# Splitting float32 weights into two float32r parts: by the vector and scalar engines, or by a casting and an adding DMA

## The chip, the cores and the metric

The kernel runs on one core of one Trainium2 chip. The metric is device time in microseconds (us) of one execution, as the median of several runs. A profile of one execution stands beside it. PE is the engine that multiplies matrices, DVE the vector engine, ACT the scalar engine, POOL the GpSimd engine; SP only issues DMAs here. Every engine runs its own instructions strictly in order.

## The reference, cut to what matters

Two layers of a decoder block over 272 tokens (16 learned ones ahead of 256) of 1024 channels. All weights and activations are float32.

```python
for l in range(2):
    h = rms_norm(x, norm1_g[l])
    u = h @ w_in[l]                       # 1024 x 6560, split among the mixers and their gates
    y_a = conv_module(u_conv, ...)        # gated depthwise convolution, layer norm, projection
    y_b = mla(c_q, c_kv, k_rope, ...)     # latent attention, 8 heads
    y_c = hgrn2(hq, hf, hi, hg, ...)      # gated linear recurrence, 4 heads
    mix = gates[0] * y_a + gates[1] * y_b + gates[2] * y_c
    x = x + mix @ w_out[l]                # 1024 x 1024
    h2 = rms_norm(x, norm2_g[l])
    x = x + square(relu(h2 @ w_ff1[l])) @ w_ff2[l]    # 1024 x 4096 and back
return x[:, 16:]
```

## The kernel before

Tokens lie along the free dimension, channels on the 128 partitions. Weights are packed on the host into blocks of 128 partitions by 1024 float32 columns (512 KB), here called *pieces*; all products with weights go piece by piece. There are 276 of them: per layer 51 of `w_in`, 2 of `w_uq`, 1 of `w_ukv`, 12 of the three branch projections, 8 of `w_out`, 32 of `w_ff1` and 32 of `w_ff2`.

To multiply in float32r and keep the accuracy, each weight and each activation is held as a high part (rounded to float32r) and a low part (the rest), and `mm3` (lines 207 to 210) adds three products into one PSUM bank: high weight by high activation (line 208), low weight by high activation (209), high weight by low activation (210). A piece has eight blocks of 128 columns, so it takes 24 matmuls of 272 columns each (256 in nearly all of layer 1, where the first 16 tokens are dropped).

`piece` (line 193) makes the parts. `fetch` (line 104) loads the raw piece by a DMA from SP into `wraw`, of which there are three buffers. ACT copies it, rounding, into `whi` (line 198). DVE subtracts, `wraw - whi`, into `wlo` (line 200). `whi` and `wlo` have four buffers each. The raw buffer comes free when DVE has subtracted; `whi` and `wlo` when the last matmul of the piece has read them. These steps run at a higher priority than their place in the program (`AHEAD`), and a scheduler sets the order in which each engine's instructions stand; the semaphores follow from that order.

In each layer a mixer stage comes first: pieces of `w_in` and of the branch projections, with the attention, recurrence and convolution steps woven in. Then comes a dense stage: `w_out`, `w_ff1`, `w_ff2`, 72 pieces in which PE does nearly nothing else. POOL does small work only: constants at the start, powers of -1/2 for the norms (`rsqrt`, line 213, and line 806), and memsets and copies in the recurrence (lines 660, 703, 754).

At the start SP loads `xT` in four parts and, in between, the first two blocks of `w_in` (lines 113 to 116), the second of which is handed to `piece` as `raw`.

Of the kernel before, what the change touches and what calls it, by code (L numbers as in the profile page):

```python
# [45 lines left out]
# Column tiles of w_in, in the order in which they are computed.  # L46
# [19 lines left out]
# Columns of the block of per-partition parameters (per layer).  # L66
# [9 lines left out]
# Columns of the block of constants.  # L76
# [10 lines left out]
def block_kernel(ctx, tc, xT_d, pp_d, cc_d, win_d, wuq_d, wukv_d, wbr_d, wout_d, wff1_d, wff2_d, out_d):  # L87
# [15 lines left out]
    # ---------------------------------------------------------------- inputs and constants  # L103
    def fetch(src, n=1024):
        raw = wsp.tile([P, 1024], F32, name="wraw", tag="wraw")
        nc.sync.dma_start(out=raw[:, :n], in_=src[:, :n])
        return raw
# [3 lines left out]
    with tc.high_priority(offset=2 * AHEAD):  # L111
        nc.scalar.dma_start(out=pp, in_=pp_d)
        for j in range(4):
            nc.sync.dma_start(out=xT[:, 2 * j:2 * j + 2, :], in_=xT_d[:, 2 * j:2 * j + 2, :])
            if j == 0:
                first = {"kr": fetch(win_d[0, 0], KD * ROPE), "kv": fetch(win_d[0, 1])}
# [60 lines left out]
    # ---------------------------------------------------------------- helpers  # L177
# [15 lines left out]
    def piece(src, raw=None):  # L193
        """1024 columns of weights, as their high and low parts in float32r."""
        with tc.high_priority(offset=AHEAD):
            raw = raw or fetch(src)
            hi = wsp.tile([P, 1024], F32R, name="whi", tag="whi", bufs=4)
            act.copy(out=hi, in_=raw)  # L198
            lo = wsp.tile([P, 1024], F32R, name="wlo", tag="wlo", bufs=4)
            dve.tensor_tensor(out=lo, in0=raw, in1=hi.bitcast(F32), op=SUB)  # L200
        return hi, lo
# [13 lines left out]
    def spread_rows(r, dst, wins, t0):  # L215
        """dst[:, t - t0] = r of token t on every partition; r holds a column for each window of tokens."""
# [10 lines left out]
    def rms_spread(sq, wcol, wins, t0, rtile=None):  # L227
        """1 / sqrt(eps + the sum over the partitions of sq * wcol) for each token, on every partition."""
# [15 lines left out]
    def add_square(dst, x, k):  # L244
        """dst becomes, or gains, x * x."""
# [11 lines left out]
    def scale_input(xg, l, k):  # L257
        """x * g, before the first norm's division."""
# [5 lines left out]
    # ---------------------------------------------------------------- lower bounds of the second layer  # L264
# [14 lines left out]
    # ---------------------------------------------------------------- layers  # L279
    for l in range(DEPTH):  # L280
# [5 lines left out]
        # h = RMSNorm(x) * g  # L286
# [51 lines left out]
        # ------------------------------------------------------------ u = h @ w_in  # L338
        tiles = win_tiles()
        def win_acc(j, n0):  # L340
            hi, lo = piece(win_d[l, j], first["kv"] if l == 0 and j == 1 else None)
# [17 lines left out]
        def rope_keys(j):  # L359
            """The shared rotary keys: 32 columns, as four sums of two of the eight terms, on 32 partitions each."""  # L360
# [58 lines left out]
        # ------------------------------------------------------------ latent projections  # L419
# [110 lines left out]
        # ------------------------------------------------------------ attention  # L530
        def attention_steps():
# [7 lines left out]
            def finish(w, po):  # L539
                """The heads' outputs for the queries of a tile, with the channels on the partitions."""  # L540
# [37 lines left out]
            def scores(w, c):  # L578
                """Of a pair of heads: exp(q k - max) / its sum."""
# [28 lines left out]
            def turned(w, pr):  # L608
                """The weights of a head, with the keys on the partitions."""
# [29 lines left out]
        # ------------------------------------------------------------ HGRN2  # L639
        def hgrn_steps():  # L640
# [16 lines left out]
            # weights of the keys s in a tile for the queries t of the same tile  # L657
# [11 lines left out]
            for hp in range(2):  # L669
# [4 lines left out]
                # blocks of 8 tokens  # L674
# [22 lines left out]
                # the later half of a block of 16, 32 or 64 tokens against its earlier half  # L697
# [32 lines left out]
                # chunks of 64 tokens against earlier chunks  # L730
# [367 lines left out]
```

## Time and profile before

| | us |
|---|---|
| time, median of 3 runs (lowest to highest) | 965.31 (964.18 to 965.49) |
| span of the profiled execution | 965.4 |
| PE busy | 954.1 |
| DVE busy | 709.2 |
| ACT busy | 521.3 |
| POOL busy | 47.0 |

The span runs from the first to the last instruction of the profiled execution; it is also all that the profile gives of that execution's own time. It stands 0.1 us above the median, within the runs' own spread, so nothing that lies around the span needs to be added. An engine's busy time is the time its instructions took; a DMA issue and a wait are not counted. The profile's windows show, for a stretch of the span, how often a line ran, TensorE's granted clock (1.00 is 2.4 GHz, 0.50 is 1.2 GHz), the mean busy share of the core's 16 DMA engines and the rate at which they moved bytes.

### The profile page before, as it was taken

How to read it: one execution, taken by the hardware profiler on the slowest of the kernel's cores; microseconds unless marked ns; L12 is line 12 of the kernel's file. 1: busy time of each engine (PE TensorE's matmuls, PEld its weight loads, DVE VectorE, ACT ScalarE, POOL GpSimd, SP SyncE). 2: the span in 40 equal slices, each digit the busy share in tenths (PEclk: the TensorE clock that was granted, in tenths of full speed). 3: DMA queues.
4: the chain of work that ended last, by engine and by line, in shares of the span. 5: the costliest groups of instructions: out<-in, count | busy, mean ns of one | idle time of the engine just before them, and what ended most of it. 6: DMA issues, size and time to landing. Idle time of an engine off the chain costs nothing.

```text
span 965.4 us, 18801 instructions
## 1 busy us (share of the span) xinstructions
PE 954.1 (99%) x7578; PEld 906.3 (94%) x7578; DVE 709.2 (73%) x1315; ACT 521.3 (54%) x941; POOL 47.0 (5%) x73
## 2 busy tenths in 40 slices
PE   7999999999999999999999999999999999999998
PEld 6989988888999999999999899888899999999998
DVE  6888998874887866655557899989759887765552
ACT  6575765543536655544436576665445566563331
POOL 2103100000000000000000021000000000000000
PEclk9999999998999999999999999999999999999999
DMA  8444333332455555555554444333334565556561
GB/s 276 149 141 153 110 111 109 110 114 84 154 173 176 175 174 176 175 175 174 175 180 153 131 154 152 107 114 111 131 122 164 161 202 192 188 184 194 192 202 60
DMA packets 42423, 149.18 MB, mean 155 GB/s; under 512 B 4704, under 2 KB 6368, under 8 KB 42336
## 3 DMA queue, kind: packets, MB, share of 16 engines
q1 hardware_dynamic: 40608, 146.10, 46.8%
q10 hardware_dynamic: 1728, 1.88, 0.6%
q8 instruction: 59, 0.97, 0.4%
q14 instruction: 28, 0.23, 0.1%
HBM read 146.91 MB, written 1.05 MB: 153 GB/s over the span
## 4 chain that ended last, share of the span: by engine, by line
PE 96%; DVE 2%; DMA 2%; ACT 1%; issue 0%; ACTq 0%
PE acc L208 18%; PE acc L210 18%; PE acc L209 18%; PE hx L208 9%; PE hx L210 9%; PE hx L209 9%; PE sm L633 2%; PE mx L588 1%; PE pt L612 1%; PE hx L714 1%; DVE wlo L200 1%; PE sm L473 1%; PE hx L797 1%; DMA wraw<-in_win_dram 1%; PE mx L836 1%; PE hx L796 1%
## 5 line engine op out<-in xcount | busy, mean ns | idle before, releaser
L200 DVE TENSOR_TENSOR wlo<-wraw,whi 128x1024 fp32r<-128x1024 f32 x276 | 337.6, 1224 | 183.8 <-ACT whi L198 183.0
L198 ACT CAST whi<-wraw 128x1024 fp32r<-128x1024 f32 x276 | 289.2, 1049 | 338.6 <-PE acc L210 187.6
L208 PE MATMUL acc<-hhi,whi 128*128 128x272 f32 (+1 forms) x704 | 208.0, 296 | 0.0
L209 PE MATMUL acc<-hhi,wlo 128*128 128x272 f32 (+1 forms) x704 | 204.3, 290 | 0.0
L210 PE MATMUL acc<-hlo,whi 128*128 128x272 f32 (+1 forms) x704 | 203.7, 290 | 0.0
L208 PEld LDWEIGHTS acc<-hhi,whi 128*128 128x128 f32 x704 | 133.7, 190 | 7.9 <-issue 4.8
L210 PEld LDWEIGHTS acc<-hlo,whi 128*128 128x128 f32 x704 | 133.5, 190 | 3.1 <-issue 1.7
L209 PEld LDWEIGHTS acc<-hhi,wlo 128*128 128x128 f32 x704 | 133.9, 190 | 1.6 <-issue 0.6
L829 DVE SCALAR_TENSOR_TENSOR cacc<-hpad,pph,cacc 128x272 f32<-128x272 f32 (+1 forms) x240 | 110.3, 486 | 0.3
L210 PE MATMUL acc<-xlo,whi 128*128 128x272 f32 (+1 forms) x256 | 73.1, 286 | 0.0
L208 PE MATMUL acc<-xhi,whi 128*128 128x272 f32 (+1 forms) x256 | 73.1, 286 | 0.0
L210 PE MATMUL hx<-xlo,whi 128*128 128x272 f32 (+1 forms) x256 | 73.0, 285 | 0.0
L209 PE MATMUL hx<-fhi,wlo 128*128 128x272 f32 (+1 forms) x256 | 72.9, 285 | 0.0
L208 PE MATMUL hx<-xhi,whi 128*128 128x272 f32 (+1 forms) x256 | 72.9, 285 | 0.0
L209 PE MATMUL acc<-xhi,wlo 128*128 128x272 f32 (+1 forms) x256 | 72.9, 285 | 0.0
L209 PE MATMUL hx<-xhi,wlo 128*128 128x272 f32 (+1 forms) x256 | 72.9, 285 | 0.0
L209 PE MATMUL acc<-fhi,wlo 128*128 128x272 f32 (+1 forms) x256 | 72.9, 285 | 0.0
L208 PE MATMUL acc<-fhi,whi 128*128 128x272 f32 (+1 forms) x256 | 72.8, 284 | 0.0
L208 PE MATMUL hx<-fhi,whi 128*128 128x272 f32 (+1 forms) x256 | 72.8, 284 | 0.0
L210 PE MATMUL hx<-flo,whi 128*128 128x272 f32 (+1 forms) x256 | 72.7, 284 | 0.0
L210 PE MATMUL acc<-flo,whi 128*128 128x272 f32 (+1 forms) x256 | 72.7, 284 | 0.0
L208 PEld LDWEIGHTS acc<-xhi,whi 128*128 128x128 f32 x256 | 48.3, 189 | 0.1
(344 smaller groups left out, 2115.6 us busy)
## 6 DMA issues: line engine op xcount, KB each, us to landing
wraw<-in_wff_dram SPq DMA_DIRECT2D x128, 512.0 KB, 4.2
wraw<-in_win_dram SPq DMA_DIRECT2D x102, 512.0 KB, 3.4
wraw<-in_wbr_dram SPq DMA_DIRECT2D x24, 512.0 KB, 3.3
wraw<-in_wout_dram SPq DMA_DIRECT2D x16, 512.0 KB, 3.4
wraw<-in_wuq_dram SPq DMA_DIRECT2D x4, 512.0 KB, 3.8
xT<-in_xT_dram SPq DMA_DIRECT2D x4, 272.0 KB, 5.1
wraw<-in_wukv_dram SPq DMA_DIRECT2D x2, 512.0 KB, 3.8
out_dram<-xT ACTq DMA_DIRECT2D x8, 128.0 KB, 3.6
```

The source lines that it names most:

```text
L198: act.copy(out=hi, in_=raw)
L200: dve.tensor_tensor(out=lo, in0=raw, in1=hi.bitcast(F32), op=SUB)
L208: pe.matmul(out, whi, xhi, start=start, stop=False)
L209: pe.matmul(out, wlo, xhi, start=False, stop=False)
L210: pe.matmul(out, whi, xlo, start=False, stop=stop)
L473: pe.matmul(sums[32 * h:32 * h + 32, :L], sel96[:QK, g, :], msq_[:QK, h, :], start=(g == 0), stop=(g == 1))
L588: pe.matmul(sh, qT[h // 4][:, h % 4, WIN[w]:WIN[w] + P], kT[h // 4][:, h % 4, :nk], start=True, stop=False)
L612: pe.transpose(pt[:WROWS[kw], 2 - kw, :], pr[:, WIN[kw]:WIN[kw] + WROWS[kw]], ident)
L633: pe.matmul(place(po, h, P), vv[kw][:WROWS[kw], h * VD:(h + 1) * VD], pts[h % 2][:WROWS[kw], 2 - kw, :], start=(kw == 0), stop=(kw == w))
L714: pe.matmul(ps[:, w - 1, h, :], kl[:, h, WIN[w]:WIN[w] + P], ql[:, h, q0:q0 + 64], start=True, stop=True)
L796: pe.matmul(o, at[w][:, h, :], vtok[w][:, hc], start=True, stop=False)
L829: dve.scalar_tensor_tensor(out=a, in0=hpad[:, c, T0 + k:T0 + k + N], scalar=hpar(l, "cw", c * CK + k), in1=a, op0=MUL, op1=ADD)
```

## The change

The raw pieces are no longer brought on chip. POOL issues a DMA from HBM straight into `whi`; since source and destination differ in type (float32, float32r), this DMA casts on the way. ACT then writes `-whi` into `wlo`, and POOL issues a second DMA from the same place in HBM that adds onto `wlo`, which leaves weight minus high part there. `whi` and `wlo` have five buffers each instead of four. DVE's subtraction is gone. `wraw` is left with one small buffer, for the 256 columns of the rotary keys that SP still loads. The first piece is no longer fetched ahead by SP. Comments and docstrings are gone too, with the line numbers kept.

```diff
     def fetch(src, n=1024):
-        raw = wsp.tile([P, 1024], F32, name="wraw", tag="wraw")
+        raw = wsp.tile([P, KD * ROPE], F32, name="wraw", tag="wraw", bufs=1)
         nc.sync.dma_start(out=raw[:, :n], in_=src[:, :n])
         return raw
...
             if j == 0:
-                first = {"kr": fetch(win_d[0, 0], KD * ROPE), "kv": fetch(win_d[0, 1])}
+                first = {"kr": fetch(win_d[0, 0], KD * ROPE)}
...
-    def piece(src, raw=None):
-        """1024 columns of weights, as their high and low parts in float32r."""
+    def piece(src):
+
         with tc.high_priority(offset=AHEAD):
-            raw = raw or fetch(src)
-            hi = wsp.tile([P, 1024], F32R, name="whi", tag="whi", bufs=4)
-            act.copy(out=hi, in_=raw)
-            lo = wsp.tile([P, 1024], F32R, name="wlo", tag="wlo", bufs=4)
-            dve.tensor_tensor(out=lo, in0=raw, in1=hi.bitcast(F32), op=SUB)
+            hi = wsp.tile([P, 1024], F32R, name="whi", tag="whi", bufs=5)
+            nc.gpsimd.dma_start(out=hi, in_=src)
+            lo = wsp.tile([P, 1024], F32R, name="wlo", tag="wlo", bufs=5)
+            act.activation(out=lo, in_=hi.bitcast(F32), func=AF.Copy, scale=-1.0)
+            nc.gpsimd.dma_start(out=lo, in_=src, accum_op=ADD)
         return hi, lo
...
-            hi, lo = piece(win_d[l, j], first["kv"] if l == 0 and j == 1 else None)
+            hi, lo = piece(win_d[l, j])
```

On POOL, near the start of the program, the constants end and the first norm's power (`r`, line 213) follows. Before (names are tiles; "waits" names whose semaphore is waited for):

```order
L663 MEMSET at_1130 16x64
L146 MEMSET d_126 128x1 [waits Pool_49]
L146 MEMSET d_126 128x1 x4
L162 CAST causal<-stage 128x128 [waits DMAHW4_49]
L163 CAST masks<-stage 128x640
L213 TENSOR_TENSOR r_195<-me,mhalf 128x3 [waits DVE_49]
L213 TENSOR_TENSOR ra<-ra,mhalf 128x6 [waits DVE_49]
```

And with the change, on the same engine at the same place (five issues of `whi` and two of `wlo` stand further up):

```order
L124 COPY ident_101<-ident 32x32 x2
L164 CAST identb<-ident 128x128 [waits Pool_49]
L200 DMA wlo<-in_win_dram 128x1024 [waits Activation_49]
L200 DMA wlo<-in_win_dram 128x1024 [waits DMASW0_49,Activation_49]
L200 DMA wlo<-in_win_dram 128x1024 [waits DMASW1_49,Activation_49]
L162 CAST causal<-stage 128x128 [waits DMAHW1_49]
L163 CAST masks<-stage 128x640
L213 TENSOR_TENSOR r_193<-me,mhalf 128x3 [waits DVE_49]
L197 DMA whi<-in_win_dram 128x1024 [waits DMASW2_49,PE_49]
L200 DMA wlo<-in_win_dram 128x1024 [waits DMASW5_49,DMASW3_49,Activation_49]
L197 DMA whi<-in_win_dram 128x1024 [waits DMASW4_49,PE_49]
```

The first norm's power now stands behind five issues of low parts, each of which waits for ACT, and each later issue of a high part waits for PE to free its buffer.

On POOL, around the dense stage of layer 0, there was nothing to do: between the second norm's inputs (line 806, then `r`) and the first memset of layer 1 (`qq`, line 352) no row stands:

```order
L806 TENSOR_TENSOR ss<-ss,mhalf 16x4 [waits DVE_49]
L806 TENSOR_TENSOR ss<-ss,mhalf 128x4 [waits DVE_49] x2
L213 TENSOR_TENSOR r<-me,mhalf 128x3 [waits DVE_49]
L352 MEMSET qq 128x4x16 [waits DVE_49,PE_49,Activation_49]
L660 MEMSET at_6969 128x512
```

Now the issues for 72 pieces stand there, two for each. In these rows of `w_ff1`, a piece's low part has its high part's number plus two (`whi_3927` and `wlo_3929` are one piece), and the pieces follow each other in steps of 35:

```order
L197 DMA whi_3822<-in_wff1_dram 128x1024 [waits DMASW7_49,PE_49]
L200 DMA wlo_3789<-in_wff1_dram 128x1024 [waits DMASW0_49,Activation_49]
L197 DMA whi_3857<-in_wff1_dram 128x1024 [waits DMASW1_49,PE_49]
L197 DMA whi_3892<-in_wff1_dram 128x1024 [waits DMASW2_49,PE_49]
L200 DMA wlo_3824<-in_wff1_dram 128x1024 [waits DMASW3_49,Activation_49]
L200 DMA wlo_3859<-in_wff1_dram 128x1024 [waits DMASW4_49,Activation_49]
L197 DMA whi_3927<-in_wff1_dram 128x1024 [waits DMASW5_49,PE_49]
L200 DMA wlo_3894<-in_wff1_dram 128x1024 [waits DMASW6_49,Activation_49]
L197 DMA whi_3962<-in_wff1_dram 128x1024 [waits DMASW7_49,PE_49]
L197 DMA whi_3997<-in_wff1_dram 128x1024 [waits DMASW0_49,PE_49]
L200 DMA wlo_3929<-in_wff1_dram 128x1024 [waits DMASW1_49,Activation_49]
```

The high part of a piece is issued one or two pieces ahead of its neighbour's low part: `wlo_3929` stands behind `whi_3997`, which belongs to the piece after the next.

On ACT in the same stage, a piece's rounding copy stood between the two activations of one tile of `w_ff1` (`rl`, line 966, and its square `fhi`, line 967) and those of the next. Before:

```order
L198 CAST whi_4620<-wraw_4618 128x1024 [waits DMAHW1_49,PE_49]
L966 ACTIVATE rl_4505<-acc_4480 128x272 [waits DVE_49]
L967 ACTIVATE fhi_3824<-rl_4505 128x272 [waits Activation_49]
L198 CAST whi_4656<-wraw_4654 128x1024 [waits DMAHW2_49,PE_49]
L966 ACTIVATE rl_4541<-hx_4516 128x272 [waits DVE_49]
```

With the change:

```order
L199 ACTIVATE wlo_4664<-whi_4662 128x1024 [waits DMASW6_49,DMASW1_49]
L966 ACTIVATE rl_4587<-hx_4562 128x272 [waits DVE_49,PE_49]
L967 ACTIVATE fhi_3750<-rl_4587 128x272 [waits Activation_49]
L199 ACTIVATE wlo_4699<-whi_4697 128x1024 [waits DMASW2_49,DMASW0_49]
L966 ACTIVATE rl_4622<-acc_4597 128x272 [waits DVE_49,PE_49]
```

The negating copy takes the place of the rounding one; it waits for two DMAs (the high part's landing, and that of the low part that had the buffer before) where the rounding one waited for a DMA and PE.

## Rows read from the trace of the kernel before

**Rows 1.** The page, busy time of each engine, share of the span, instructions.

```profile
PE 954.1 (99%) x7578; PEld 906.3 (94%) x7578; DVE 709.2 (73%) x1315; ACT 521.3 (54%) x941; POOL 47.0 (5%) x73
```

**Rows 2.** The page, the chain that ended last, share by engine.

```profile
PE 96%; DVE 2%; DMA 2%; ACT 1%; issue 0%; ACTq 0%
```

**Rows 3.** PE's waits: line waited for, us in total, times, longest.

```profile
PE hx L368 <- DVE wkr L364: 6.1, 1, 6.1
PE hx L208 <- DVE gate L889: 0.9, 1, 0.9
```

**Rows 4.** Windows for line 198: length, ACT busy (times), clock, DMA share, GB/s.

```profile
0.00:20.00 20.00, 6.26 (x6) 1.00 0.85 286
20.00:100.00 80.00, 22.21 (x22) 1.00 0.47 147
100.00:230.00 130.00, 28.05 (x27) 0.97 0.33 108
230.00:270.00 40.00, 11.56 (x11) 1.00 0.46 149
270.00:485.00 215.00, 74.36 (x71) 1.00 0.54 174
485.00:545.00 60.00, 18.87 (x18) 1.00 0.48 161
545.00:665.00 120.00, 30.30 (x29) 1.00 0.39 127
665.00:745.00 80.00, 21.20 (x22) 1.00 0.42 134
745.00:950.00 205.00, 75.36 (x72) 1.00 0.59 186
```

**Rows 5.** The page, costliest groups: busy us, mean ns, idle before.

```profile
L200 DVE TENSOR_TENSOR wlo<-wraw,whi 128x1024 fp32r<-128x1024 f32 x276 | 337.6, 1224 | 183.8 <-ACT whi L198 183.0
L198 ACT CAST whi<-wraw 128x1024 fp32r<-128x1024 f32 x276 | 289.2, 1049 | 338.6 <-PE acc L210 187.6
```

**Rows 6.** Timeline of ACT, dense stage of layer 0: start, length, instruction.

```profile
350.00 1.05 ACT L198 CAST whi<-wraw 128x1024 fp32r<-128x1024 f32 x1 [1.22 <-PE hx L210]
350.95 0.39 ACT L966 ACTIVATE rl<-hx 128x272 f32<-128x272 f32 x1
351.38 0.43 ACT L967 ACTIVATE fhi<-rl 128x272 fp32r<-128x272 f32 x1
353.03 1.05 ACT L198 CAST whi<-wraw 128x1024 fp32r<-128x1024 f32 x1 [1.22 <-PE acc L210]
```

**Rows 7.** The page, SP's DMA queue (packets, MB, share) and one issue line.

```profile
q1 hardware_dynamic: 40608, 146.10, 46.8%
...
wraw<-in_wff_dram SPq DMA_DIRECT2D x128, 512.0 KB, 4.2
```

**Rows 8.** First window: engines' busy time (instructions), clock, DMA share, GB/s.

```profile
0.00:10.00 10.00, 3.90 (x18) 1.08 (x19) 5.11 (x18) 6.63 (x14) 4.27 (x33) 1.00 0.83 292
```

**Rows 9.** Tile wraw, SP's issues: times, duration in ns min/median/max.

```profile
L106 SPq DMA_DIRECT2D wraw<-in_wff_dram x128: 327/328/775, 294.4 to 944.0; - x128
```

**Rows 10.** Groups on POOL, its longest instruction: busy us, mean ns.

```profile
L213 POOL TENSOR_TENSOR rq<-rq,mhalf 128x24 f32<-128x24 f32 (+1 forms) x2 | 8.0, 3986 | 9.7 <-DVE rq L485 9.7
```

**Rows 11.** Windows in the mixer of layer 0, columns as in rows 8.

```profile
216.00:218.00 2.00, 2.00 (x11) 1.40 (x11) 0.55 (x3) 0.24 (x1) 0.00 (x0) 1.00 0.56 156
220.00:222.00 2.00, 2.00 (x10) 2.00 (x10) 0.92 (x2) 0.32 (x1) 0.62 (x1) 0.50 0.00 0
```

**Rows 12.** Timeline of PE there: two matmuls that follow each other.

```profile
222.50 0.43 PE L208 MATMUL acc<-hhi,whi 128*128 128x272 f32 x1
222.73 0.43 PE L209 MATMUL acc<-hhi,wlo 128*128 128x272 f32 x1
```

## The prediction

> **What bounds the kernel now.** I read the busy times first. PE is busy for 954.1 of 965.4 us, 99% of the span; DVE for 73%, ACT for 54%, POOL for 5% [rows 1]. The chain that ended last says the same: 96% of it is PE [rows 2]. So PE's own work sets the end, and what the other engines save is worth something only where PE waits for them. It hardly does: its waits add up to little more than the 6.1 us at the start, until the rotary keys' weights are there [rows 3]. PE's whole idle time is 965.4 - 954.1 = 11.3 us; no edit that leaves the matmuls alone can win more.
>
> Next, how fast pieces are used, stretch by stretch [rows 4]. Line 198 runs once for each piece, so a stretch's length over its count is the time that PE gives to a piece: 3.64 us in 20 to 100, 4.81 in 100 to 230 (other mixer work lies between), 3.64 to 270, 3.03 in the dense stage of layer 0 (215 / 71), then 3.33, 4.14, 3.64, and 2.85 in the dense stage of layer 1 (205 / 72). The DMA share in the same rows goes from 0.33 to 0.59, at one load of 512 KB for each piece. That is the resource that the change loads.
>
> **What is removed.** DVE loses 276 subtractions of 1224 ns, 337.6 us [rows 5]. They lie beside the matmuls, so I count nothing for them; at most a part of PE's 11.3 us could come back. SP's loads go away and reappear on POOL.
>
> **What ACT does instead.** The rounding copy takes 1049 ns, 276 times [rows 5]. The negating copy has the same shape and count; I take 1049 ns again, no change. It now waits for a DMA that POOL issued, with the next tile's two activations behind it in ACT's order. Those two take 0.39 and 0.43 us, and ACT is done with a piece in under 2 us of 3.03 [rows 6]. PE waits for them when its PSUM banks run out; with four banks in turn that comes after the missing weights themselves, so nothing on top. If that cover is gone, ACT's 1.05 us joins each late piece's path.
>
> **What the DMA engines must do.** SP's queue moved 146.10 MB in 46.8% of 16 engines' span [rows 7]: 451.8 us, or 3.09 us for each MB, 1.62 us for one piece of 0.524 MB. I call this a pass. Now the high part is one pass. The low part is a second pass from HBM, and since it adds, the old value of its destination has to be read as well. No row shows an adding DMA, so I bound it: one pass if that reading costs the engines nothing, two if it costs as much as reading from HBM. That makes 3.24 or 4.86 us for a piece. I take two passes, hence 4.86 us, since the bytes read are doubled and nothing in a row excludes that they count. Casting I take at the plain rate, for lack of a row; a slower cast lengthens the first pass.
>
> The Trainium skill, "Collectives: The Full Stack", the section on the bandwidth ceiling and the fold count, says that an add in the DMA engines is slow not for its arithmetic but because it needs two source reads on one ring, which halves the rate. No run here shows it yet; by it the low part is two passes, the value taken above.
>
> The sum: wherever PE gives a piece less than 4.86 us, the piece now takes 4.86. Times the counts of rows 4: 20 to 100, 22 x 4.86 - 80 = 27; 100 to 230, 1; to 270, 13; dense stage of layer 0, 71 x 4.86 - 215 = 130; then 27, 21, 27; dense stage of layer 1, 72 x 4.86 - 205 = 145. Together 392 us. Five buffers hide none of it, since a stretch lasts tens of pieces. The first 20 us hold 6 pieces at a share of 0.85, so 17.0 us of the engines, of which 9.7 are pieces and 7.3 `xT` and constants; 6 x 4.86 + 7.3 = 36.5, 16 more. 965.4 + 392 + 16 = **1373 us**. The span stands 0.1 above the median of the runs, so this is also the forecast of the time.
>
> **What the order on POOL adds.** POOL is strictly in order, and its issues are now 552. A low part stands behind the high part of the piece after the next, which waits until PE has left the buffer five pieces back. From there PE has two pieces' time until it needs that low part, and in it lie: two issues, the pass of the high part ahead, and the low part's landing. A plain load takes 4.2 us from issue to landing in the dense stages [rows 7]; with one pass more, 5.82. With g for an issue, a piece takes at least (2g + 1.62 + 5.82) / 2 = g + 3.72. An issue on SP takes 0.33 us [rows 9], which gives 4.05, below 4.86. POOL issues no DMA in the trace; its longest instruction takes 3.99 us [rows 10], the upper end. I take a value nearer to SP's, because it is the same request; then the DMA engines remain the later limit. From g = 1.14 us this loop decides instead, and at 2.43 POOL alone is full with two issues for each piece.
>
> POOL's own 47 us [rows 1] now stand among these issues, and about 36 of its rows in the mixers wait for another engine, holding the issues behind them. I count 0, since the mixers' pieces come at 3.6 to 4.8 us anyway; at worst each costs a piece, 36 x 4.86 = 175 us, which goes into the range. The first norm's power stands behind five low parts at the start; its wait is inside the 16 us.
>
> **Rivals.** *Two passes are enough*: the adding costs no more than a plain load. Then 3.24 us for a piece hurts only the dense stages, 71 x 3.24 - 215 = 15 and 72 x 3.24 - 205 = 28, and 10 at the start: 1018 us. With the order on POOL at 3.6 us it is 100 and 10: 1075. For it: the first window moved 292 GB/s at a share of 0.83 [rows 8], so full engines could do 352, a pass of 1.49; then even three passes make only 4.47, and 295 + 14 = 1274 in all. Against it: the old value must come from somewhere.
>
> The Trainium skill, "DMA: Bandwidth & Descriptors", the specifications, gives a ceiling of 435 GB/s at the SBUF ports. As an estimate from that figure, three passes would take 3.61 us, and the time would be about that of this rival's upper end. No row here comes near that rate.
>
> *POOL's issues decide*: g is well above SP's 0.33. At g = 1.9 the loop takes 5.6 us for a piece, and the sum of rows 4 at 5.6 is 593: 965 + 593 + 20 = 1578 us. At 3.99 POOL alone takes 7.98 us, the sum is about 1240, the time 2230. For it: POOL writes its requests by program, SP does not; its small powers take microseconds [rows 10]. Against it: nothing in the trace gives a price.
>
> *TensorE's clock falls in the gaps*: PE would work 3.03 of 4.86 us. In the trace the granted clock went from 1.00 in 216 to 218, where 11 small matmuls filled 2 us, to 0.50 in 220 to 222 [rows 11], and the matmuls behind it came at 0.23 us instead of some 0.125 (3.03 / 24) [rows 12]. That is 24 x 0.23 = 5.5 us for a piece, more than 4.86: PE would bound again at the lower clock, with 5.5 to 5.6 in both dense stages and the mixers held up as well, some 1550 us. Against it: each piece still brings 24 dense matmuls.
>
> *Not slower*: the engines' share counts waiting inside a transfer, and both loads fit beside each other. This decides if high part, low part and old value take together no more than 2.85 us, that is 0.95 us for each pass of three (550 GB/s), or 1.42 for two (368). The highest rate in a row is 292 [rows 8]. Then the time is 954 to 967.
>
> **How the numbers follow.** Forecast, three passes, 1250 to 1500: 0.42. Two passes, or three at a rate above the rows', 1010 to 1250: 0.18. POOL's issues or the clock, 1500 to 2000: 0.26. Over 2000, where POOL is near its upper end or an adding transfer costs more than two passes: 0.10. Not slower: 0.04, half of it faster. The range leaves out the last two cases, 0.14: 1010 to 2000 us. The likeliest case's own range, 1250 to 1500, stands beside it. About 0.2% (2 us) is what a measurement of this kernel can tell from no change; faster 0.02, same 0.02, slower 0.96.
>
> **What would show it.** Right: in the windows of the dense stages some 4.9 us for each piece in both layers alike, though layer 1 has fewer columns; the DMA share there above 0.9; PE waiting for the low part's landing, not the high part's; DVE near 370 us busy; ACT's line 199 near 1.05 us. Wrong in size: a share near 0.6 with PE waiting means that latency and order bound it, so POOL's issue time or the loop; a granted clock of 0.5 in the dense stages means the clock rival; a dense stage still at 3.03 us for a piece means that the transfers were hidden after all. Two passes would show as a landing of the low part no longer than that of the high part.

## The result and the profile after

The changed kernel takes 1256.66 us (median of 3 runs, 1253.51 to 1264.56) against 965.31 before: a ratio of 1.3034, 95% interval 1.2984 to 1.3083. The forecast was 1373 us; the time lies in its range, 116 us below the likeliest value. The span of the profiled execution is 1254.6 us, 289.2 more than before.

From the page of the changed kernel: busy time of each engine, POOL's DMA queue (packets, MB, share of 16 engines), the chain that ended last by engine, the costliest groups on ACT and POOL (busy us, mean ns, idle before), and the DMA issues with the time to landing.

```profile
PE 1044.3 (83%) x7578; PEld 964.6 (77%) x7578; DVE 405.6 (32%) x1039; ACT 525.4 (42%) x941; POOL 438.5 (35%) x625
...
q0 software_dynamic: 79488, 289.44, 96.8%
...
issue 46%; POOL 23%; DMA 18%; PE 7%; ACT 3%; DVE 1%; POOLq 0%; ACTq 0%; DVEq 0%
...
L199 ACT ACTIVATE wlo<-whi 128x1024 fp32r<-128x1024 f32 x276 | 291.8, 1058 | 567.8 <-DMA whi<-in_win_dram 219.6
...
L200 POOL DMA_DIRECT2D wlo<-in_wff_dram x128 | 113.9, 890 | 244.3 <-ACT wlo L199 212.6
...
L197 POOL DMA_DIRECT2D whi<-in_wff_dram x128 | 86.3, 674 | 106.2 <-PE acc L210 53.1
...
whi<-in_wff_dram POOLq DMA_DIRECT2D x128, 512.0 KB, 7.5
wlo<-in_wff_dram POOLq DMA_DIRECT2D x128, 512.0 KB, 7.4
```

PE was 99% of the span and 96% of the chain [rows 1, 2]; now it is 83% and 7%. The 46% of the chain called `issue` is time for which the chain names no wait; POOL's 438.5 us of busy time include its DMA issues, 552 of its 625 instructions. The queue that carries the weights fills 96.8% of the engines' span, where SP's filled 46.8% [rows 7]; a landing takes 7.5 us in place of 4.2. DVE did lose its 300 us, and ACT's group costs what it cost [rows 5]; e8 below shows that neither moves the end.

Who waits for what, in the same kernel: PE's longest waits (us in total, times, longest), then POOL's.

```profile
PE acc L209 <- DMA wlo<-in_wff_dram: 52.7, 43, 3.0
PE hx L209 <- DMA wlo<-in_wff_dram: 49.6, 38, 2.9
PE acc L209 <- DMA wlo<-in_win_dram: 27.1, 18, 4.0
```

```profile
POOL wlo L200 <- ACT wlo L199: 330.3, 151, 7.3
POOL whi L197 <- PE acc L210: 129.2, 60, 6.1
POOL wlo L200 <- ACT gate L873: 84.8, 25, 7.0
POOL whi L197 <- PE hx L210: 77.6, 34, 6.1
```

PE waits for low parts (line 209), hardly for high parts; before it waited for next to nothing, 6.1 us at the start [rows 3]. POOL, which now issues every weight, waits 330 us for ACT's negation and 85 for the step `gate` that stands before it on ACT, and 207 us for PE to free high parts.

To see where the 289 us lie I cut the run near the ends of the stages, at piece 65, 136, 204 and 275, on a grid of 4 us, by the counts of line 198 before and 199 after. The last 17 us before and 19 us after lie behind these cuts.

| stage (pieces) | before, us | after, us | more | predicted |
|---|---|---|---|---|
| start and mixer 0 (65) | 268 | 324 | 56 | 16 + 27 + 1 + 13 = 57 |
| dense 0 (71) | 216 | 296 | 80 | 130 |
| mixer 1 (68) | 264 | 324 | 60 | 27 + 21 + 27 = 75 |
| dense 1 (71) | 200 | 292 | 92 | 145 |

The rows of the two dense stages, as in rows 4 (length, ACT busy with its times, granted clock, DMA share, GB/s), of the changed kernel:

```profile
324.00:620.00 296.00, 75.12 (x71) 0.95 1.04 252
944.00:1236.00 292.00, 75.18 (x71) 0.94 1.05 259
```

That is 4.17 and 4.11 us for a piece, alike in both layers as predicted, but not 4.86.

### The profile page after: what moved, and what is told of

It reads as the page before. It is cut to its first block, busy times and chain, and to the rows that moved or that the text cites. A ratio compares the mean times of both kernels' runs of the same rounds, so it can differ in the third digit from the quotient of the medians.

```text
span 1254.6 us, 19026 instructions
## 1 busy us (share of the span) xinstructions
PE 1044.3 (83%) x7578; PEld 964.6 (77%) x7578; DVE 405.6 (32%) x1039; ACT 525.4 (42%) x941; POOL 438.5 (35%) x625
## 3 DMA queue, kind: packets, MB, share of 16 engines
q0 software_dynamic: 79488, 289.44, 96.8%
HBM read 291.62 MB, written 1.05 MB: 233 GB/s over the span
## 4 chain that ended last, share of the span: by engine, by line
issue 46%; POOL 23%; DMA 18%; PE 7%; ACT 3%; DVE 1%; POOLq 0%; ACTq 0%; DVEq 0%
POOL wlo L200 12%; POOL whi L197 10%; DMA whi<-in_win_dram 9%; DMA whi<-in_wff_dram 4%; DMA wlo<-in_win_dram 2%; ACT wlo L199 2%; PE acc L209 2%; PE acc L208 1%; PE acc L210 1%; DMA whi<-in_wbr_dram 1%; DMA wlo<-in_wff_dram 1%; DMA whi<-in_wout_dram 1%; PE sm L633 0%; PE mx L588 0%; DVE cacc L829 0%
## 5 line engine op out<-in xcount | busy, mean ns | idle before, releaser
L199 ACT ACTIVATE wlo<-whi 128x1024 fp32r<-128x1024 f32 x276 | 291.8, 1058 | 567.8 <-DMA whi<-in_win_dram 219.6
L209 PE MATMUL acc<-hhi,wlo 128*128 128x272 f32 (+1 forms) x704 | 211.5, 300 | 19.4 <-DMA wlo<-in_win_dram 19.3
L200 POOL DMA_DIRECT2D wlo<-in_wff_dram x128 | 113.9, 890 | 244.3 <-ACT wlo L199 212.6
L200 POOL DMA_DIRECT2D wlo<-in_win_dram x102 | 91.1, 894 | 246.8 <-ACT gate L873 79.1
L210 PEld LDWEIGHTS acc<-hlo,whi 128*128 128x128 f32 x704 | 138.7, 197 | 0.8 <-issue 0.5
L197 POOL DMA_DIRECT2D whi<-in_wff_dram x128 | 86.3, 674 | 106.2 <-PE acc L210 53.1
L209 PE MATMUL acc<-fhi,wlo 128*128 128x272 f32 (+1 forms) x256 | 79.5, 311 | 29.4 <-DMA wlo<-in_wff_dram 29.4
L197 POOL DMA_DIRECT2D whi<-in_win_dram x102 | 73.6, 735 | 61.5 <-PE acc L210 52.8
L968 DVE TENSOR_TENSOR rl<-rl 128x272 f32<-128x272 f32 (+1 forms) x64 | 27.4, 431 | 192.6 <-ACT fhi L967 192.6
L209 PEld LDWEIGHTS acc<-fhi,wlo 128*128 128x128 f32 x256 | 52.5, 205 | 34.8 <-DMA wlo<-in_wff_dram 34.8
```

The costliest lines, as they stand in the source:

```text
L197: nc.gpsimd.dma_start(out=hi, in_=src)
L199: act.activation(out=lo, in_=hi.bitcast(F32), func=AF.Copy, scale=-1.0)
L200: nc.gpsimd.dma_start(out=lo, in_=src, accum_op=ADD)
L209: pe.matmul(out, wlo, xhi, start=False, stop=False)
L210: pe.matmul(out, whi, xlo, start=False, stop=stop)
L968: dve.tensor_tensor(out=rl[:, :N], in0=rl[:, :N], in1=rl[:, :N], op=MUL)
```

## The experiments

Times of single executions stand without an interval; only the change, e2 and e4 ran more than once. The kernel before ran beside them at 965.17 to 967.08 us. "Dense" is the time for a piece in the two dense stages, cut as above (a step of the grid is 0.06 us for a piece). A *pass* is again the engines' time for 512 KB: a queue's share times the span over 276.

| run | edit | us | dense 0, 1 | mixer 0, 1 (us) |
|---|---|---|---|---|
| the change | | 1256.66 | 4.17, 4.11 | 324, 324 |
| e8_cast_alone | no adding DMA | 964.12 | 2.99, 2.87 | 268, 264 |
| e1_plain_second | second DMA does not add | 1042.00 | 3.32, 3.32 | 280, 272 |
| e4_cast_and_subtract | before, high part by casting DMA | 1004.77 | 3.21, 3.15 | 280, 260 |
| e5_raw_and_add | before, low part by adding DMA | 1177.73 | 3.89, 3.89 | 300, 308 |
| e6_add_from_sbuf | as e5, the add reads SBUF | 1389.82 | 4.90, 4.90 | 328, 348 |
| e11_sbuf_four_raw | as e6, four raw buffers | 1233.87 | 4.23, 4.17 | 316, 304 |
| e2_six_buffers | six buffers of each part | 1194.32 | 3.83, 3.77 | 324, 312 |
| e7_half_add | half of each add | 1159.91 | 3.94, 4.00 | 288, 292 |
| e9_half_add_six | half, six buffers | 1155.84 | 3.89, 3.83 | 292, 300 |
| e10_raw_half_add | as e5, half | 1053.29 | 3.32, 3.32 | 288, 276 |
| e12_half_add_six_four | half, six high, four low | 1003.87 | 3.15, 3.15 | 276, 264 |
| e13_six_and_four | six high, four low | 1147.65 | 3.77, 3.83 | 300, 288 |

### What each pass costs

**e8_cast_alone.** The changed kernel without its second DMA.

```diff
-            nc.gpsimd.dma_start(out=lo, in_=src, accum_op=ADD)
```

> Only the casting DMA is left; the low part is the negated high part as ACT writes it (the adding DMA is left out, so the low parts are wrong). One casting pass for a piece. All theories: PE sets the end again, 965 to 985. What it measures is the price of a casting pass: if casting costs the engines nothing, the DMA share over the span is near the 46.8% of the kernel before (1.62 us for a piece); if the share is 60% or more, the high part's pass is itself dearer than the plain load, and the adding pass is the rest of 4.2 to 4.4 us.

Measured 964.12 us, beside 965.17 for the kernel before. From its page:

```profile
PE 949.0 (99%) x7578; PEld 903.7 (94%) x7578; DVE 404.4 (42%) x1039; ACT 533.3 (55%) x941; POOL 191.0 (20%) x349
...
q0 software_dynamic: 39744, 144.72, 49.7%
```

A casting pass is 0.497 x 962.0 / 276 = 1.73 us, against 1.62 for SP's plain one. All the loss comes with the second DMA, and relieving DVE of 300 us gains nothing that can be measured.

**e1_plain_second.** The second DMA writes instead of adding.

```diff
-            nc.gpsimd.dma_start(out=lo, in_=src, accum_op=ADD)
+            nc.gpsimd.dma_start(out=lo, in_=src)
```

> The second DMA of each piece no longer adds: it loads the same piece a second time into the low part (so the low part holds the weight itself; this part of the computation is changed). Same instructions, same order on POOL, same bytes from HBM. Theory A (the DMA engines' time for a piece is the limit, and an adding transfer takes more of it than a plain one): the dense stages go from 4.0 us for a piece to two plain passes, 3.2, or to PE's own pace of 3.0, and the time to 1010 to 1080. Rival B (HBM's rate at some 255 to 270 GB/s is the limit): nothing changes, 1255. Rival C (order on POOL and latency of the two DMAs in a row): the low part lands earlier by what adding costs; 1100 to 1200 with the DMA share well under 0.9.

Measured 1042.00 us. The same issues in the same order, the same bytes read from HBM: 215 us of the 291 go away with the adding itself; the other 77 stay with a second DMA that does not add. POOL's issue of the second DMA falls too, from 0.89 to 0.53 us on the mean; e5 below, in which POOL has half of the issues, shows that this is not the main part. The queue's row and one dense stage:

```profile
q0 software_dynamic: 79488, 289.44, 87.1%
```

```profile
280.00:516.00 236.00, 75.63 (x72) 1.00 0.98 314
```

0.871 x 1039.9 / 552 = 1.64 us for a pass, and 314 GB/s.

**e4_cast_and_subtract.** The kernel before, with `whi` brought by a casting DMA from POOL in place of ACT's copy; SP still loads the raw piece and DVE subtracts.

```diff
-            act.copy(out=hi, in_=raw)
+            nc.gpsimd.dma_start(out=hi, in_=src)
```

> Half of the change alone: the high part by the casting DMA from HBM, but the raw piece is still loaded by SP and DVE still subtracts for the low part. Two plain passes for a piece, nothing adds, and no transfer waits for another one. Theory A (the adding costs the engines more than a plain pass, and the two transfers of a piece stand in a row): at some 1.7 us of engine time for a pass two passes fit under 3.0 us as long as neither waits for the other; the dense stages keep 3.0 to 3.1 us and the time is 965 to 990. Rival B (two loads for each piece are already too much for HBM or the engines, as 3.3 us for a piece with the plain second load suggests): 1030 to 1050.

Measured 1004.77 us, ratio 1.0403 (1.0383 to 1.0422). That lies between the two ranges expected. Two plain passes for each piece, on two queues, are mostly hidden: they cost 39 us. Windows of line 200, the second inside dense 1:

```profile
768.00:992.00 224.00, 86.78 (x72) 0.98 0.98 337
820.00:980.00 160.00, 65.91 (x55) 0.99 1.02 355
```

In that second stretch a piece takes 160 / 55 = 2.91 us at 355 GB/s: close to PE's own pace of 2.85. So two reads from HBM and the cast explain at most a small part of the 291 us.

**e5_raw_and_add.** The kernel before, with ACT's negation and the adding DMA in place of DVE's subtraction. POOL issues only low parts; SP loads raw pieces.

```diff
-            dve.tensor_tensor(out=lo, in0=raw, in1=hi.bitcast(F32), op=SUB)
+            act.activation(out=lo, in_=hi.bitcast(F32), func=AF.Copy, scale=-1.0)
+            nc.gpsimd.dma_start(out=lo, in_=src, accum_op=ADD)
```

> The other half alone: SP loads the raw piece and ACT rounds it into the high part, as before; then ACT negates it and a DMA adds the piece onto it from HBM. One plain pass and one adding pass, as with the whole change, without a cast on the first. Theory A: the engines' time for a piece is that of the whole change, 3.7 us or more in the dense stages, 1190 to 1290 in all. Rival: the casting was the dear part of the first pass; then 1100 or less.

Measured 1177.73 us, a little under the 1190 to 1290 expected. Here each kind of pass has its own queue (q0 adds, q1 is plain), so the prices come apart; then dense 0:

```profile
q0 software_dynamic: 39744, 144.72, 65.3%
q1 hardware_dynamic: 40608, 146.10, 33.2%
```

```profile
300.00:576.00 276.00, 74.24 (x71) 0.99 1.04 271
```

An adding pass is 0.653 x 1175.6 / 276 = **2.78 us**, the plain one beside it 1.41. Together 4.19 us at a share of 1.04: 4.0 us for a piece, measured 3.89. With no high part on POOL at all, this points to a floor of the engines; e2 and e13 below come to 3.8 with other buffers and another order.

**e6_add_from_sbuf** and **e11_sbuf_four_raw.** Does the second read from HBM matter? The add takes the raw piece from SBUF instead.

```diff
-            nc.gpsimd.dma_start(out=lo, in_=src, accum_op=ADD)
+            nc.gpsimd.dma_start(out=lo, in_=raw, accum_op=ADD)
```

> As the run with the raw piece and the adding DMA, but the adding DMA reads the raw piece that already lies on chip instead of HBM: HBM is read once for each piece, the DMA engines move as much as before. Theory A (the engines' time, not HBM's rate): as that run within 5%, 1180 to 1290. Rival B (HBM): one load for each piece as in the kernel before, under 1060.

Measured 1389.82 us: slower than e5, so the expectation of about e5's time was missed. The run mixed two things, since the raw buffer is now held until the add has landed: by its page 5.4 us for the load, 1.05 and 1.06 for ACT's two steps, 0.87 for the issue and 6.2 for the landing, 14.6 us over three buffers, or 4.9 us for a piece. That is the measured 4.90. A fourth raw buffer (five fewer gate buffers make room) takes that away:

```diff
-        raw = wsp.tile([P, 1024], F32, name="wraw", tag="wraw")
+        raw = wsp.tile([P, 1024], F32, name="wraw", tag="wraw", bufs=4)
...
-NGATE = 15
+NGATE = 10
```

> The kernel of e6_add_from_sbuf, in which the adding DMA reads the raw piece in SBUF, with four raw buffers instead of three (and ten buffers of gate tiles instead of fifteen, to make room). Theory, the raw buffer was the limit there, since it is held from the issue of its load until the add has landed, about 14.9 us: 14.9 / 4 = 3.7, and the engines, at 2.87 + 1.40 us of transfer for a piece, give about 4.0; so 3.9 to 4.1 us in the dense stages and 1210 to 1260 us in all. Rival, an add from SBUF is itself the slower transfer: 4.6 to 4.8 us for a piece as before, 1350 to 1400 us.

Measured 1233.87 us, inside the 1210 to 1260 expected; dense 4.23 and 4.17, a little over the expected 3.9 to 4.1. The queues and the HBM line of e11:

```profile
q0 software_dynamic: 39744, 144.72, 63.1%
q1 hardware_dynamic: 40608, 146.10, 33.7%
...
HBM read 146.91 MB, written 1.05 MB: 120 GB/s over the span
```

With half the reads from HBM, the adding pass still costs 0.631 x 1231.9 / 276 = 2.82 us. So the price is in the adding, and not in the second read from HBM.

### What the order on POOL costs

**e2_six_buffers.** Six buffers for each part instead of five (`NGATE = 10` for room).

```diff
-            hi = wsp.tile([P, 1024], F32R, name="whi", tag="whi", bufs=5)
+            hi = wsp.tile([P, 1024], F32R, name="whi", tag="whi", bufs=6)
...
-            lo = wsp.tile([P, 1024], F32R, name="wlo", tag="wlo", bufs=5)
+            lo = wsp.tile([P, 1024], F32R, name="wlo", tag="wlo", bufs=6)
```

> Six buffers for each part instead of five; for the room, 10 gates are computed ahead instead of 15, which shifts work inside the mixers but not in the dense stages. Theory A (DMA engines): the dense stages stay at 4.0 us for a piece, the share at 1.03 to 1.07, the time at 1240 to 1260. Rival C (latency: five buffers leave four pieces' time for issue, landing, negating, issue, landing, 17 us by the medians): one more piece of slack, 17 over 5, brings the dense stages to 3.4 us and the time under 1130.

Measured 1194.32 us, ratio 1.2368 (1.2331 to 1.2406), between the two ranges expected. Dense stages of 3.83 and 3.77 us:

```profile
324.00:596.00 272.00, 75.88 (x72) 0.99 1.08 274
908.00:1176.00 268.00, 74.21 (x70) 0.98 1.08 278
```

This is about e5's floor, reached by another route: one plain and one adding pass take 3.8 us, at a share of 1.08 (the share adds up the times of packets, so above 1 packets overlap on an engine). The change stands 0.3 us above that floor in the dense stages, and much further in the mixers, which six buffers hardly help (324 and 312 us; 324 and 324 in the change).

**e7_half_add** and **e9_half_add_six.** The adding DMA on half of the columns, with five and with six buffers (e9 with `NGATE = 10`, as e2).

```diff
-            nc.gpsimd.dma_start(out=lo, in_=src, accum_op=ADD)
+            nc.gpsimd.dma_start(out=lo[:, :512], in_=src[:, :512], accum_op=ADD)
```

> The adding DMA covers 512 of the 1024 columns; the other half of the low part keeps the negated high part (so that half of the low parts is left wrong). Theory A: a piece costs the engines the high part's pass and half the adding pass, under PE's 3.0 and 2.85 us if adding is the dearer one; the dense stages return to PE's pace or 3.1, the time to 980 to 1050. Rival B (bytes from HBM, 1.5 passes at some 260 GB/s): 3.0 us for a piece, the same. Rival C (latency): the landing of the low part shortens by a part of its transfer only; above 3.4 us for a piece, 1080 to 1180.

> The adding DMA on 512 of 1024 columns, now with six buffers (half of the low parts is left wrong). With five buffers a piece took 3.8 us in the dense stages at a DMA share of 0.78. If the wait of the two transfers for each other set that, one more buffer takes it to 3.1 us or to PE's pace, the time to 990 to 1060. If an adding transfer costs the engines nearly the same however short it is, it stays at 3.6 us or more, 1120 and over.

Measured 1159.91 and 1155.84 us, dense stages at 3.9 to 4.0 and 3.8 to 3.9: e7 in the range of latency, e9 in that of a transfer whose price its size hardly changes, which e12 and e10 put to the test. (The expectation of e9 has 3.8 us and 0.78 for e7; over the whole of dense 0 it is 3.94 and 0.87.) First e7, then e9:

```profile
288.00:568.00 280.00, 75.19 (x71) 0.98 0.87 203
```

```profile
292.00:568.00 276.00, 75.16 (x71) 0.98 0.87 203
```

The engines are no longer full, at 203 GB/s, and a piece hardly gets cheaper; the sixth buffer, from which I expected a gain in e9, brings 0.1 to 0.2 us. So buffers are not the limit there, and neither is the loop of the prediction (a low part behind a high part that waits for PE): a sixth buffer gives that loop one piece's time more.

What I had not counted stands in the order on POOL. A low part's issue waits for ACT's negation, which waits for the landing of its own high part, and all later issues, the next high parts among them, stand behind that wait. With k high parts issued (its own included) before a low part goes out, a piece takes at least the way from one high part's issue to its low part's, divided by k. In e7 and e9, k is 2 in most of the dense pieces: e7's landing of 6.0 us, 1.06 for ACT, 0.87 for the issue, 7.9 / 2 = 4.0 us. In the changed kernel k is 2 or 3 by turns in the dense stages and mostly 2 in the mixers. Counted over POOL's timelines, the mean k is 2.5 and 2.6 in the dense stages of the change and 2.1 in its mixers, 2.0 to 2.25 in e7 and e9, and 3.0 to 3.1 in e12 and e13 below. The change's timelines in dense 0 (start, length, instruction, idle before and what ended it), POOL first, then ACT:

```profile
457.96 0.55 POOL L197 DMA_DIRECT2D whi<-in_wff_dram  x1 [2.52 <-PE hx L210]
459.79 0.85 POOL L200 DMA_DIRECT2D wlo<-in_wff_dram  x1 [1.28 <-ACT wlo L199]
461.32 0.55 POOL L197 DMA_DIRECT2D whi<-in_wff_dram  x1 [0.68 <-PE acc L210]
464.35 0.54 POOL L197 DMA_DIRECT2D whi<-in_wff_dram  x1 [2.47 <-PE hx L210]
464.88 0.91 POOL L200 DMA_DIRECT2D wlo<-in_wff_dram  x1
```

```profile
463.28 1.06 ACT L199 ACTIVATE wlo<-whi 128x1024 fp32r<-128x1024 f32 x1 [1.36 <-DMA whi<-in_wff_dram]
```

A high part goes out at 457.96, ACT has it at 463.28, its low part goes out at 464.88: 6.9 us, in which two more high parts were issued (k = 3). POOL waits for ACT and for PE in turn.

**e12_half_add_six_four** and **e13_six_and_four** change the split of the buffers, and by it the order: six buffers for high parts and four for low ones, the same memory as the change. The scheduler then places a low part later, and k is 3 nearly everywhere. (Where the two expectations say "three pieces further", the piece itself is counted.) On POOL, from layer 1, the change:

```
L197 DMA whi_9414<-in_wff1_dram 128x1024
L200 DMA wlo_9381<-in_wff1_dram 128x1024
L197 DMA whi_9449<-in_wff1_dram 128x1024
L197 DMA whi_9484<-in_wff1_dram 128x1024
L200 DMA wlo_9416<-in_wff1_dram 128x1024
L200 DMA wlo_9451<-in_wff1_dram 128x1024
```

and e13, where each `wlo` stands behind the `whi` two pieces on (`whi_9379` and `wlo_9381` are one piece):

```
L197 DMA whi_9449<-in_wff1_dram 128x1024
L200 DMA wlo_9381<-in_wff1_dram 128x1024
L197 DMA whi_9484<-in_wff1_dram 128x1024
L200 DMA wlo_9416<-in_wff1_dram 128x1024
L197 DMA whi_9519<-in_wff1_dram 128x1024
L200 DMA wlo_9451<-in_wff1_dram 128x1024
```

```diff
-            hi = wsp.tile([P, 1024], F32R, name="whi", tag="whi", bufs=5)
+            hi = wsp.tile([P, 1024], F32R, name="whi", tag="whi", bufs=6)
...
-            lo = wsp.tile([P, 1024], F32R, name="wlo", tag="wlo", bufs=5)
+            lo = wsp.tile([P, 1024], F32R, name="wlo", tag="wlo", bufs=4)
```

> The kernel of e7_half_add with six buffers for high parts and four for low parts instead of five and five: the same memory, and the same part left out (of the last 512 columns of a piece the low part stays minus the high part). What it changes is the order on POOL: a low part's issue now stands behind the high part of three pieces further, in place of two. Theory, the order on POOL: a piece takes the time from issue to issue of a high part's landing, ACT's negation and the low part's issue, divided by the number of high parts under way: (0.55 + 6.0 + 1.06 + 0.87) / 3 = 2.8 us, so PE's own time or the engines' 3.1 us decide; 985 to 1050 us. Rival, the adding transfer has a price that its size hardly changes: 3.7 us or more for a piece, 1130 us or more.

Measured 1003.87 us, against 1159.91 with the same half add in the old order: inside the range that the theory of the order gave. The sixth high buffer alone does not do it: e9 has six high buffers too, with six low ones, the old order and ten gates, and takes 1155.84. POOL's two longest waits for ACT of e7, then dense 0 of e12 and the same waits there:

```profile
POOL wlo L200 <- ACT wlo L199: 296.9, 133, 7.0
POOL wlo L200 <- ACT rl L966: 146.2, 59, 5.7
```

```profile
276.00:500.00 224.00, 76.15 (x73) 0.99 1.04 253
```

```profile
POOL wlo L200 <- ACT wlo L199: 120.7, 105, 3.7
...
POOL wlo L200 <- ACT rl L966: 73.3, 60, 2.9
```

> The changed kernel with six buffers for high parts and four for low parts, so the same memory and the whole computation; on POOL a low part then stands behind the high part three pieces further throughout, where five and five gave two or three in turn. Theory, the order on POOL with the DMA engines just under it: the dense stages go from 4.0 to the floor of 3.7 to 3.8 us for a piece that e2_six_buffers showed, 1185 to 1215 us. Rival, the number of low buffers or the engines alone set it: 1240 to 1280 us.

Measured 1147.65 us, below the expected 1185 to 1215. The dense stages stand on the floor, as expected (its queue and dense 0):

```profile
q0 software_dynamic: 79488, 289.44, 102.0%
```

```profile
300.00:568.00 268.00, 75.11 (x71) 1.00 1.08 279
```

The rest was gained in the mixers, 300 and 288 us against 324 and 324, which the expectation had left out. e2, whose k is still 2.2 and 2.4 on the mean there, kept 324 and 312 (it also computes ten gates ahead and not fifteen, which no run takes apart). For the mixers of the change the loop gives at least (6.9 for the landing + 1.06 + 0.89) / 2 = 4.4 us for a piece; 324 / 65 = 5.0 was measured, with ACT's and POOL's other steps in the same two queues.

**e10_raw_half_add.** e5 with the half add, to see that a half transfer does save something where no high part stands behind a low one.

```diff
-            nc.gpsimd.dma_start(out=lo, in_=src, accum_op=ADD)
+            nc.gpsimd.dma_start(out=lo[:, :512], in_=src[:, :512], accum_op=ADD)
```

> The kernel of e5_raw_and_add, with the adding transfer on the first 512 columns of a piece only. Part of the computation is left out: of the other 512 columns the low part stays minus the high part. Theory, the order on POOL: here SP loads the raw pieces, so no high part stands behind a low part on POOL, and the half transfer should at last save something. Plain pass 1.40 us, half adding pass about 1.4: 2.8 us of the engines for a piece, so PE's own 2.85 to 3.03 us come back nearly everywhere; 975 to 1030 us in all. Rival, an adding transfer has a price for each piece that its size hardly changes: the dense stages stay at 3.6 us for a piece or more; 1120 us or more.

Measured 1053.29 us: between the two, nearer to the theory. Its queues give 0.428 x 1051.1 / 276 = 1.63 us for the half adding pass and 0.401 x 1051.1 / 276 = 1.53 for the plain one. Half the columns cost 0.59 of the whole add, not half, so there is a part that its size does not change, but it is small; I had put it at nothing. The sum of 3.16 us is more than the 2.8 expected, but it is not shown to be what keeps PE's 2.85 to 3.03 from coming back: the engines stand at a share of 0.92 and 0.93 in the dense stages, where e12 reached 1.04. The queues and the two dense stages of e10:

```profile
q0 software_dynamic: 39744, 72.37, 42.8%
q1 hardware_dynamic: 40608, 146.10, 40.1%
```

```profile
288.00:524.00 236.00, 74.61 (x72) 0.99 0.92 236
800.00:1036.00 236.00, 74.47 (x72) 0.97 0.93 239
```

What holds e10 at 3.3 us for a piece stays open.

## Why the prediction was right in direction and too high

**What bounds before, what DVE is worth, what ACT costs: right.** e8 has DVE at 404 us and the time of before. ACT's line 199 takes 1058 ns, 1049 were assumed.

**The cast at the plain rate: right.** 1.73 us in e8, and 1.62 in e4 (0.447 x 1002.1 / 276), against 1.62.

**The adding pass as two passes: the ratio nearly held, the sum of 4.86 us was too large, twice over.** The adding pass was put at 3.24 us; e5 shows 2.78. That is 1.7 of SP's passes of the kernel before (1.62), but 2.0 of the plain ones beside it in e5 (1.41), and 1.9 in e11 (2.82 against 0.337 x 1231.9 / 276 = 1.50). So the pass of 1.62, read from a queue with room, was larger than the plain pass of e5, where the engines are full: e5's two passes add up to 4.19, and the change's own queue gives 0.968 x 1254.6 / 276 = 4.40. And a piece's two transfers were simply added up, as if a share of 1.00 were the end; in e2, e5 and e13 the engines' share goes to 1.04 to 1.08 and a piece takes 3.8 to 3.9 us, some 1.0 less than forecast. By 3.8 the dense stages alone give 71 x 3.8 - 215 = 55 and 72 x 3.8 - 205 = 69 in place of 130 and 145; e13 has 52 and 72. (The counts of [rows 4] come to 278, since two copies lie across the edges of windows; that made the forecast some 10 us too long.)

The Trainium skill, "Collectives: The Full Stack", the section on the bandwidth ceiling and the fold count, puts a ReduceScatter between cores at half the rate of an AllGather, because its add needs two source reads. Here, on one core, an adding pass runs at 0.51 of the plain rate beside it (1.41 / 2.78, e5) and at 0.58 of that of the kernel before (1.62 / 2.78): the trace agrees in direction, and nearly in size. e11 adds that a source in SBUF makes it no cheaper.

**The order on POOL: named, but the wrong loop.** The step counted a low part behind a high part that waits for PE, g + 3.72, and found it below the engines. Issues cost 0.67 and 0.89 us on the mean in the dense stages, under the 1.14 from which that loop was to decide, so that part of the step was fair. Fair too was the 0 for POOL's own rows: they wait for other engines for 22.5 us in all, the issues for 779. What it left out is the other direction, a high part behind a low part that waits for its own high part's landing and ACT. By e13 the order, with the split of the buffers that sets it, costs 1257 - 1148 = 109 us, 60 of it in the mixers (24 and 36 us), where I had counted 0, and 28 and 20 in the dense stages.

**The mixer sums, 57 and 75 against 56 and 60, came near by luck.** They were worked out at 4.86 us of the engines for a piece. At 3.8 the same sums come to 15 us (with the start) and 12. The order on POOL gave back most of the rest: e13, which has the same transfers, loses 32 and 24 us there, 24 and 36 less than the change. One error covered the other in the mixers; in the dense stages the smaller transfer shows, and there lie 103 of the 118 us between forecast and span (50 and 53; the other 15 are in mixer 1).

**The rivals.** *Two passes are enough* is out: that is e1 at 1042 us, inside the 1018 to 1075 that it was given (by its own sum 1015, for 6 x 3.24 + 7.3 - 20 is 7 and not 10), and the change lies 215 us above it. *POOL's issues decide* is out by their price, 0.67 and 0.89 us against the 1.14 it needs. *TensorE's clock*: the granted clock dips, 0.95 and 0.94 in the dense stages where before had 1.00 [rows 4], and PE's busy time grows from 954 to 1044 us; but PE is idle for 210 us beside that, and waits for low parts. In e13 the clock is 1.00 and 0.99 in the dense stages and they still take 3.8 us. *Not slower* is out.

**What would show it.** The share above 0.9, both layers alike, PE waiting for low parts came as said, and DVE roughly (405.6 us, where 370 was given); 4.9 us for a piece did not. That a low part's landing is no longer than a high part's (7.4 and 7.5 us) was to be the sign of two cheap passes. It was a bad sign: both stand in the same full queue, and a landing there measures the queue and not the transfer.

**What stays open.** In the dense stages of the change, five buffers also give 4.1 us: a buffer's whole round (0.67 + 7.5 + 1.06 + 0.89 + 7.4 + PE's 3.0) is 20.5 us, over five. e2 and e13 change the buffers and the order there at once, so how the 0.3 us above the floor divide is not told apart. In the mixers e2 against e13, six high buffers in both, points to the order. Why the mixers of e13 still lose 32 and 24 us, and where e1's 77 us lie, was not taken apart, nor was the effect of the clock's dips on the waits. No version tried is faster than the kernel before beyond what can be measured.

## What to carry to other kernels

Price a DMA that adds as a transfer of its own, 1.7 to 2.0 plain ones here, and lay the sum beside what the consumer gives a piece: work that an idle engine does for nothing is lost when it moves to a resource that is half full. On an in-order engine that issues both halves of a chain, follow the wait in both directions, and count how many of the first halves are under way before a second half blocks the queue; the split of the buffers between the two can set that number at no cost in memory (1257 to 1148 us here). When a partial sum comes out right, ask whether the same term, at its measured size, would still give it.

## What the runs showed of the hardware

- An adding DMA of 512 KB from HBM onto SBUF took 2.78 us of the 16 engines (e5), a plain or casting one 1.41 (e5, at a share of 1.04) to 1.73 (e8, alone); reading the addend from SBUF instead gave 2.82 (e11).
- One plain and one adding stream together did not go under 3.8 us for a piece (271 to 279 GB/s, share 1.04 to 1.08, in e2, e5 and e13), while two plain ones reached 355 GB/s and 2.91 us (e4). The highest rate before was 292 GB/s [rows 8].
- Issuing a DMA of 128 rows took POOL 0.53 us for a casting one in e8 and 0.67 on the mean beside adding ones in the change, and 0.89 for an adding one, against 0.33 on SP [rows 9].
